# A two-layer decoder trunk on one core: q, k, v, cross-query and memory projections in chunks of 512 columns

## The chip, the core and the metric

The kernel runs on one core of a Trainium2 chip. The core has engines that run side by side, each through its own list of instructions in order: TensorE (matrix products; PE in the profile, with its weight loads as PEld), VectorE (DVE), ScalarE (ACT), GpSimd (POOL) and SyncE (SP), which here only issues DMAs. Data lies in SBUF, results of matrix products in PSUM, which has eight banks of 128 partitions by 512 fp32 numbers. The metric is the device time of one execution in microseconds (us). Lower is better.

## What is computed

Two layers, each on 512 tokens of width 1024, in fp32:

```python
h = rmsnorm(x, g_mix[l])
dq, dk, dv, c_q, c_kv_kr, xq, gate_logits = split(h @ w_in[l])
y_diff = diff_attention(dq, dk, dv, ...) @ w_diff_o[l]        # 8 heads, causal, two softmax maps a head
y_mla  = latent_attention(c_q, c_kv_kr, ...) @ w_mla_o[l]     # 8 heads, causal
mem_n  = rmsnorm(mem, mem_gain[l])                            # 256 memory tokens
y_mem  = memory_cross_attention(xq, mem_n, w_mem_kv[l], ...) @ w_cross_o[l]   # 4 heads
gates  = sigmoid(gate_logits + b_gate[l])                     # three gates
x = x + (gates0*y_diff + gates1*y_mla + gates2*y_mem) @ w_out[l]
u = rmsnorm(x, g_mlp[l]) @ w_mlp1[l]
x = x + square(relu(u)) @ w_mlp2[l]
```

In diff_attention each of q and k is normalized and rotated (rotary) in groups of 64 columns, a head of q or k has two such groups, and a head of v has 128 columns. In the cross-attention q and k are normalized in groups of 128 columns.

## The kernel before

**Precision.** A product of two fp32 matrices is made of three products of a faster type (fp32r). Each operand is split in hi (a rounded copy, ScalarE, line 101 or 105) and lo (the rest, VectorE, line 102 or 106), and `mm3` (lines 108 to 111) issues hi·hi, hi·lo and lo·hi into the same PSUM bank. So almost all of TensorE's work stands on lines 109 to 111, and one product of 128 rows (k) by 128 stationary columns is three matmul instructions, each with a weight load of its own.

**Two forms of projection.** Gates, output projections and the MLP hold 128 columns of the weights stationary and stream all 512 tokens: 512 columns an instruction. The projections of this change (q, k, v, cross-query xq, memory k and v) hold a block of 128 tokens of h stationary and stream weight columns: `chunk256` (lines 259 to 277) does 256 columns of the weights at a time. In it one PSUM bank of the pool `acc` (two banks) takes two token blocks, 256 columns each, so the four token blocks of x need both banks (`tp` 0 and 1) and the two blocks of mem need one. A chunk is two entries, `u` 0 and 1, each with half of the eight k blocks and one weight unit; an entry goes through both banks. At the end of entry 1 `done(tp, bank)` takes the results out: for q and k (`diff_chunk`, lines 552 to 594) a copy on ScalarE (563), squares (565), sums (567), a power on GpSimd (132), rotary on VectorE (582 to 584), the normalization (586), four transposes on TensorE (590) and the split in hi and lo (593); for v a scaled copy (560). There are twelve such chunks a layer for q, k and v (three for each of four pairs of heads), two for xq (`xq_chunk`), and four for the memory (`mem_chunk`).

**Weights.** Each weight unit is at most 128 x 1024 numbers (512 KB). `load_raw` issues its DMA on SyncE into one of RB = 3 raw buffers, `do_split` makes hi and lo in one of NB = 4 pairs of buffers, in the order in which the entries use them. An entry takes its units and gives them back when its matmuls are done (lines 883 to 895). The four lines that fix the order are:

```python
while len(splits) < min(len(units), consumed + NB):
    ...
    do_split()
e.fn(splits[consumed:consumed + n])
```

**Order of the work.** A layer is a list of entries. `merge` mixes attention units (one block of queries of a head or of a pair of heads) with projection entries, phase by phase, as `PLAN` (line 25) says: latent attention with the x gates and the memory projections; then with xq and d0 (q, k and v of head pair 0); cross-attention with d1 and ym; diff attention of pairs 0 to 3 with the rest (gc, d2, d3, gd). A planner then fixes each engine's list: it takes the entries' order as priority and lets a later instruction of an engine go ahead of an earlier one that isn't ready. It also hands out the buffers of each pool: `B` (22 of 128 x 512) for q, k, v and gates, `scr` (5) for the normalization's temporaries, PSUM pools `acc` (2 banks), `s` (3), `tp` (2) and `o` (1).

**Start.** Small inputs come by DMA: `gc` on ScalarE's queue, `posi`, `fr` and `gr` (the q and k gains, which `build_rope` multiplies into the rotary tables), and later `lvt`, on GpSimd's queue (lines 122 to 129 and 185).

Of the kernel before, what the change touches and what calls it, by code (L numbers as in the profile page):

```python
# [15 lines left out]
P = 128  # L16
# [23 lines left out]
class Entry:  # L40
    def __init__(self, fn, units=()):
        self.fn, self.units = fn, list(units)
# [17 lines left out]
def tile_trunk(ctx: ExitStack, tc: tile.TileContext, x_t, mem_t, mem_n, pos, ifr, gcol, grow, w_ck, w_cq, w_kvb, w_qb,  # L60
# [7 lines left out]
    RB, NB = 3, 4  # L68
# [3 lines left out]
    pools = {n: pool(n, b) for n, b in (("H", 16), ("O", 16), ("X", 8), ("G", 1), ("B", 22), ("scr", 5), ("PT", 2))}  # L72
# [52 lines left out]
    G.dma_start(out=posi, in_=pos)  # L125
    fr = ct("fr", [P, 32])
    G.dma_start(out=fr, in_=ifr.partition_broadcast(P))
    gr = ct("gr", [P, L, 128])
    G.dma_start(out=gr, in_=grow[:, 0:128].partition_broadcast(P))
# [8 lines left out]
    dgain = ct("dgain", [P, L])  # L138

    def trig():  # L140
# [44 lines left out]
        G.dma_start(out=lvt.rearrange("p (l d) -> p l d", l=L), in_=grow[:, 128:384].partition_broadcast(P))  # L185
        for l in range(L):
# [8 lines left out]
            V.tensor_scalar(dgain[:, l:l + 1], gc[:, l, C_DO:C_DO + 1], (1.0 - lam_init) * math.sqrt(128.0), None, ALU.mult)  # L195
            V.tensor_scalar(hb[:, l, :], gc[:, l, C_B:C_B + 24], 0.5, None, ALU.mult)
# [3 lines left out]
    def mem_stats():  # L200
# [13 lines left out]
        V.tensor_scalar(mst["eps"], ms, EPS, None, ALU.mult)  # L214
# [44 lines left out]
    def chunk256(units_of, h_of, ntok, done):  # L259
        state = {}  # L260

        def part(u):
            def fn(w):
                hh = h_of()
                if u == 0:
                    state["ps"] = [ps("acc") for _ in range(ntok // 2)]
                for tp in range(ntok // 2):
                    for kk in range(4):
                        k = 4 * u + kk
                        for ti in range(2):  # L270
                            o = state["ps"][tp][:, ti * 256:(ti + 1) * 256]
                            mm3(o, hh(k, 2 * tp + ti), (w[0][0][:, kk, :], w[0][1][:, kk, :]), k == 0 and ti == 0, k == KT - 1 and ti == 1)
                    if u == 1:
                        done(tp, state["ps"][tp])
            return fn

        return [Entry(part(u), [units_of[:, 4 * u:4 * u + 4, :]]) for u in range(2)]

    def layer(l):
# [3 lines left out]
        def build_rope():  # L283
            for qk in range(2):
                a = sm.tile([P, NT, 64], F32, tag=f"ra{qk}", name=nm("ra"), bufs=1)
                b = sm.tile([P, NT, 64], F32, tag=f"rb{qk}", name=nm("rb"), bufs=1)
                for half in range(2):
                    g = gr[:, l, qk * 64 + half * 32:qk * 64 + (half + 1) * 32].unsqueeze(1).broadcast_to([P, NT, 32])
                    G.tensor_tensor(out=a[:, :, half * 32:(half + 1) * 32], in0=cosd, in1=g, op=ALU.mult)
                    G.tensor_tensor(out=b[:, :, (1 - half) * 32:(2 - half) * 32], in0=(sind if half == 0 else nsind), in1=g, op=ALU.mult)  # L290
                s["rope", qk] = (a, b)
# [45 lines left out]

        def mem_chunk(c):
            def done(tp, q):
                if c < 2:  # L340
                    y = tl("scr")
                    A.activation(out=y, in_=q, func=AF.Copy)
                    z = tl("scr")
                    A.activation(out=z, in_=y, func=AF.Square)
                    ss = small("ss", 8, 4)
                    V.tensor_reduce(out=ss[:, :4], in_=z.rearrange("p (g d) -> p g d", d=128), axis=AX.X, op=ALU.add)
                    e = small("e", 8, 4)
                    V.scalar_tensor_tensor(out=e[:, :4].rearrange("p (t h) -> p t h", t=2), in0=ss[:, :4].rearrange("p (t h) -> p t h", t=2), scalar=1.0 / 128,
                                           in1=mst["eps"].unsqueeze(2).broadcast_to([P, 2, 2]), op0=ALU.mult, op1=ALU.add)
                    f = small("f", 8, 4)  # L350
                    rsq(f[:, :4], e[:, :4], 4)
                    yv = y.rearrange("p (g d) -> p g d", d=128)
                    V.tensor_tensor(out=yv, in0=yv, in1=f[:, :4].unsqueeze(2).broadcast_to([P, 4, 128]), op=ALU.mult)
                    tp_ = ps("tp")
                    for h in range(2):
                        for t in range(2):
                            T.transpose(tp_[:, h * 256 + t * P:h * 256 + (t + 1) * P], in_=yv[:, t * 2 + h, :], identity=ident)
                    o = tl("B")
                    scale_to(o, tp_, col(C_CK))
                    s["mk"].append(o)  # L360
                else:
                    o = tl("B")
                    for t in range(2):
                        A.activation(out=o[:, t * 256:(t + 1) * 256], in_=q[:, t * 256:(t + 1) * 256], func=AF.Copy, scale=mst["r"][:, t:t + 1])
                    s["mv"].append(o)
            return chunk256(w_mem[l, c], mem_h, 2, done)
# [610 lines left out]
```

## Time and profile before

| | before |
|---|---|
| time, median of 3 runs | 2054.7 us (2052.78 to 2055.78) |
| span of the profiled execution | 2047.5 us |
| TensorE matmuls (PE) busy | 2025.8 us, 11280 instructions |
| VectorE (DVE) busy | 1125.5 us, 2058 instructions |
| ScalarE (ACT) busy | 870.5 us, 1607 instructions |
| GpSimd (POOL) busy | 152.4 us, 125 instructions |
| HBM read | 175.06 MB, 88 GB/s over the span |

The span is that of one execution, from its first to its last instruction; the time of a run also has what lies around it. A row of matmuls in the views shows the start of one instruction and its own length. Matmuls are pipelined: the next one starts while the one before still runs, so the length of one (0.28 us for 256 columns) is more than it adds to the time. What it adds is read from the distance between two starts.

### The profile page before, as it was taken

What the parts mean: (1) busy time and instruction counts of PE and PEld (TensorE: products, weight loads), DVE (VectorE), ACT (ScalarE), POOL (GpSimd) and SP (SyncE); (2) the same over time, 40 slices, a digit from 0 to 9 for tenths busy, and PEclk for the clock granted to TensorE, in tenths of its full rate; (3) what the DMA queues carried; (4) which work ended last, traced back from release to release, by engine and by line L of the source; (5) the groups of instructions that cost most, each with busy time, mean ns of one, the idle gap of its engine ahead of it and who ended that gap; (6) DMA issues with size and microseconds to landing.
All of it is one profiled execution on the core that took longest, in us unless ns stands there. A gap on an engine that the chain in (4) does not pass through costs nothing.

```text
span 2047.5 us, 28283 instructions
## 1 busy us (share of the span) xinstructions
PE 2025.8 (99%) x11280; PEld 1735.7 (85%) x11280; DVE 1125.5 (55%) x2058; ACT 870.5 (43%) x1607; POOL 152.4 (7%) x125
## 2 busy tenths in 40 slices
PE   8999999999999999999999999999999999999999
PEld 7889997888878888888888999978897788888887
DVE  7754665667656443443457546657685554434442
ACT  6565543444443442322345645444454334323221
POOL 2300110101100000000003001101020000000000
PEclk9999999999999999999999999999999999999999
DMA  5242122222214333333333321212222233333332
GB/s 178 78 140 74 63 65 60 73 73 63 73 48 150 96 97 94 102 93 101 118 95 94 115 72 63 67 58 73 73 63 63 92 124 93 94 102 93 101 94 73
DMA packets 54036, 181.09 MB, mean 88 GB/s; under 512 B 6176, under 2 KB 6704, under 8 KB 53904
## 3 DMA queue, kind: packets, MB, share of 16 engines
q1 hardware_dynamic: 51840, 175.66, 28.0%
q10 hardware_dynamic: 1872, 3.21, 0.5%
q8 instruction: 89, 1.46, 0.3%
q0 software_dynamic: 192, 0.41, 0.1%
q14 instruction: 43, 0.35, 0.1%
HBM read 175.06 MB, written 4.19 MB: 88 GB/s over the span
## 4 chain that ended last, share of the span: by engine, by line
PE 97%; ACT 1%; DMA 1%; DVE 1%; issue 0%; SPq 0%; POOL 0%; POOLq 0%; ACTq 0%
PE psacc L109 21%; PE psacc L110 20%; PE psacc L111 20%; PE pss L109 7%; PE pss L110 7%; PE pss L111 7%; PE pso L642 4%; PE pss L609 3%; PE pss L612 2%; PE pstp L638 2%; PE pstp L649 1%; PE pstp L590 1%; PE pstp L478 1%; DMA X<-in_x_t_dram 0%; DMA B<-in_mem_n_dram 0%; PE pstp L236 0%
## 5 line engine op out<-in xcount | busy, mean ns | idle before, releaser
L101 ACT ACTIVATE whi<-wraw 128x1024 fp32r<-128x1024 f32 (+3 forms) x320 | 334.5, 1047 | 726.8 <-PE psacc L110 354.5
L102 DVE TENSOR_TENSOR wlo<-wraw,whi 128x1024 fp32r<-128x1024 f32 (+3 forms) x320 | 386.0, 1207 | 103.1 <-ACT whi L101 101.8
L109 PE MATMUL psacc<-H,whi 128*128 128x512 f32 x816 | 322.0, 395 | 1.3 <-ACT B L560 1.3
L110 PE MATMUL psacc<-H,whi 128*128 128x512 f32 x816 | 321.1, 393 | 0.0
L111 PE MATMUL psacc<-H,wlo 128*128 128x512 f32 x816 | 319.6, 392 | 0.0
L109 PE MATMUL psacc<-whi,H 128*128 128x256 f32 (+1 forms) x928 | 272.8, 295 | 7.2 <-ACT whi L101 5.8
L110 PE MATMUL psacc<-wlo,H 128*128 128x256 f32 (+1 forms) x928 | 265.9, 287 | 0.5 <-DVE wlo L102 0.5
L111 PE MATMUL psacc<-whi,H 128*128 128x256 f32 (+1 forms) x928 | 265.4, 287 | 0.0
L109 PE MATMUL pss<-O,whi 128*128 128x512 f32 x640 | 249.4, 391 | 1.6 <-ACT O L105 1.6
L110 PE MATMUL pss<-O,whi 128*128 128x512 f32 x640 | 249.7, 390 | 0.0
L111 PE MATMUL pss<-O,wlo 128*128 128x512 f32 x640 | 249.4, 390 | 0.0
L109 PEld LDWEIGHTS psacc<-whi,H 128*128 128x128 f32 x928 | 176.9, 191 | 15.6 <-ACT whi L101 6.0
L109 PEld LDWEIGHTS psacc<-H,whi 128*128 128x128 f32 x816 | 153.3, 188 | 34.7 <-ACT B L560 1.7
L110 PEld LDWEIGHTS psacc<-H,whi 128*128 128x128 f32 x816 | 153.3, 188 | 32.4 <-issue 1.5
L111 PEld LDWEIGHTS psacc<-H,wlo 128*128 128x128 f32 x816 | 153.3, 188 | 32.4 <-issue 1.5
L110 PEld LDWEIGHTS psacc<-wlo,H 128*128 128x128 f32 x928 | 177.6, 191 | 3.2 <-issue 1.4
L111 PEld LDWEIGHTS psacc<-whi,H 128*128 128x128 f32 x928 | 177.0, 191 | 0.0
L808 DVE TENSOR_TENSOR X<-psacc,X 128x512 f32<-128x512 f32 x64 | 44.3, 692 | 207.1 <-PE psacc L111 207.1
L109 PEld LDWEIGHTS pss<-O,whi 128*128 128x128 f32 x640 | 120.0, 188 | 28.3 <-ACT O L105 2.0
L110 PEld LDWEIGHTS pss<-O,whi 128*128 128x128 f32 x640 | 120.2, 188 | 25.2 <-DVE O L106 0.5
L111 PEld LDWEIGHTS pss<-O,wlo 128*128 128x128 f32 x640 | 120.2, 188 | 24.5
L626 ACT ACTIVATE P<-pss,nmx 128x128 f32<-128x128 f32 (+2 forms) x224 | 115.2, 521 | 51.3 <-DVE nmx L623 44.0
(223 smaller groups left out, 3139.6 us busy)
## 6 DMA issues: line engine op xcount, KB each, us to landing
wraw<-in_w_dram SPq DMA_DIRECT2D x128, 512.0 KB, 3.6
wraw<-in_w_g_dram SPq DMA_DIRECT2D x48, 512.0 KB, 3.6
wraw<-in_w_d_dram SPq DMA_DIRECT2D x48, 512.0 KB, 3.8
wraw<-in_w_mem_dram SPq DMA_DIRECT2D x16, 512.0 KB, 3.9
wraw<-in_w_od_dram SPq DMA_DIRECT2D x16, 512.0 KB, 3.5
wraw<-in_w_out_dram SPq DMA_DIRECT2D x16, 512.0 KB, 3.8
X<-in_x_t_dram SPq DMA_DIRECT2D x16, 256.0 KB, 6.3
wraw<-in_w_xq_dram SPq DMA_DIRECT2D x8, 512.0 KB, 3.8
```

The costliest lines, as they stand in the source:

```text
L101: A.activation(out=hi, in_=src, func=AF.Copy)
L102: V.tensor_tensor(out=lo, in0=src, in1=hi, op=ALU.subtract)
L109: T.matmul(o, lhsT=l[0], rhs=r[0], start=first, stop=False)
L110: T.matmul(o, lhsT=l[0], rhs=r[1], start=False, stop=False)
L111: T.matmul(o, lhsT=l[1], rhs=r[0], start=False, stop=last)
L478: T.transpose(tp_[:96, t * P:(t + 1) * P], in_=src[t][:, h * 96:(h + 1) * 96], identity=ident)
L609: T.matmul(sw[m][:, :max(N, 256)], lhsT=qk[m][0][a], rhs=qk[m][1][b], start=i == 0, stop=i == 2)
L612: T.matmul(sv[m], lhsT=qk[m][0], rhs=qk[m][1], start=True, stop=True)
L626: A.activation(out=pt[:, m, :N], in_=sv[m], func=AF.Exp, bias=nmx[:, m:m + 1], accum_out=ssum[m])
L638: T.transpose(tp_[:, n * P:(n + 1) * P], in_=pt[:, m, j * P:(j + 1) * P], identity=ident)
L642: T.matmul(o_out[m], lhsT=w[:, n * P:(n + 1) * P], rhs=vs[m](j), start=j == 0, stop=j == nb - 1)
L808: V.tensor_tensor(out=xt, in0=q, in1=xt, op=ALU.add)
```

## The change

- **Chunks of 512 columns.** `chunk512` takes the place of `chunk256`. A bank of `acc` now holds one token block by 512 columns. For the 512 tokens of x a chunk is four entries: two passes `tp` over pairs of token blocks, each with the two halves `u` of k. A unit is now two k blocks by 512 columns (128 x 1024 numbers as before), so a chunk has four units. They are loaded and split once and kept through both passes: an entry has an offset `off`, a count `need` and a count `take` of units given back, and only the second pass gives back, two units an entry. For the memory (two token blocks) there is one pass.
- **Contents.** A chunk of q and k of a pair of heads (`qk_chunk`, 256 columns of each) and, for every second pair, a chunk of v of two pairs (`v_chunk`): d0 = q, k of pair 0 and v of pairs 0 and 1; d1 = q, k of pair 1; d2 = q, k of pair 2 and v of pairs 2 and 3; d3 = q, k of pair 3. xq is one chunk, the memory two (k, then v).
- **Taking out.** `evict(t, bank)` works on one token block of 512 columns, `done(tp)` does the transposes of a pass. The rotary step multiplies q and k together (two instructions of 512 columns in place of four of 256), and the swap of halves moves from the first product to the sum. The gains of q and k are scaled so that one `tensor_scalar` adds the epsilon for all eight groups (`gr` times 8, `ck11`, and epsilon times 128).
- **Buffers.** NB 4 to 5, `B` 22 to 24, `scr` 5 to 6; the space that GpSimd's DMAs keep is set to 2048.
- **Start.** `posi`, `fr`, `gr` and `lvt` move from GpSimd's queue to ScalarE's; one VectorE instruction scales `gr`.
- The layouts of w_mem, w_xq and w_d are laid for the new units.

```diff
 class Entry:
-    def __init__(self, fn, units=()):
-        self.fn, self.units = fn, list(units)
+    def __init__(self, fn, units=(), off=0, need=None, take=None):
+        self.fn, self.units, self.off = fn, list(units), off
+        self.need = len(self.units) if need is None else need
+        self.take = self.need if take is None else take
...
-    RB, NB = 3, 4
+    RB, NB = 3, 5
...
-    pools = {n: pool(n, b) for n, b in (("H", 16), ("O", 16), ("X", 8), ("G", 1), ("B", 22), ("scr", 5), ("PT", 2))}
+    pools = {n: pool(n, b) for n, b in (("H", 16), ("O", 16), ("X", 8), ("G", 1), ("B", 24), ("scr", 6), ("PT", 2))}
...
-    G.dma_start(out=posi, in_=pos)
+    A.dma_start(out=posi, in_=pos)
...
-    G.dma_start(out=gr, in_=grow[:, 0:128].partition_broadcast(P))
+    A.dma_start(out=gr, in_=grow[:, 0:128].partition_broadcast(P))
+
+    V.tensor_scalar(gr[:, :, 64:128], gr[:, :, 64:128], 8.0, None, ALU.mult)
...
-    def chunk256(units_of, h_of, ntok, done):
+    def chunk512(units_of, h_of, ntok, evict, done):
         state = {}
 
-        def part(u):
+        def part(tp, u):
             def fn(w):
                 hh = h_of()
                 if u == 0:
-                    state["ps"] = [ps("acc") for _ in range(ntok // 2)]
-                for tp in range(ntok // 2):
-                    for kk in range(4):
-                        k = 4 * u + kk
-                        for ti in range(2):
-                            o = state["ps"][tp][:, ti * 256:(ti + 1) * 256]
-                            mm3(o, hh(k, 2 * tp + ti), (w[0][0][:, kk, :], w[0][1][:, kk, :]), k == 0 and ti == 0, k == KT - 1 and ti == 1)
+                    state["ps"] = [ps("acc") for _ in range(2)]
+                for ti in range(2):
+                    q = state["ps"][ti]
+                    for j in range(2):
+                        for kk in range(2):
+                            k = 4 * u + 2 * j + kk
+                            mm3(q, hh(k, 2 * tp + ti), (w[j][0][:, kk, :], w[j][1][:, kk, :]), k == 0, k == KT - 1)
                     if u == 1:
-                        done(tp, state["ps"][tp])
+                        evict(2 * tp + ti, q)
+                if u == 1:
+                    done(tp)
             return fn
 
-        return [Entry(part(u), [units_of[:, 4 * u:4 * u + 4, :]]) for u in range(2)]
+        r, n = [], ntok // 2
+        for tp in range(n):
+            for u in range(2):
+                un = [units_of[:, 4 * u + 2 * j:4 * u + 2 * j + 2, :] for j in range(2)] if tp == 0 else []
+                r.append(Entry(part(tp, u), un, 0 if tp == n - 1 else 2 * u, 2, 2 if tp == n - 1 else 0))
+        return r
...
-        def diff_chunk(p, c):
+        def qk_chunk(p):
+            def evict(t, q):
...
-                for ti in range(2):
-                    yv = y[:, ti * 256:(ti + 1) * 256].rearrange("p (g b d) -> p g b d", g=4, b=2)
...
-                    V.tensor_tensor(out=zv, in0=yv[:, :, ::-1, :], in1=tab(b_), op=ALU.mult)
-                    V.tensor_tensor(out=yv, in0=yv, in1=tab(a_), op=ALU.mult)
-                V.tensor_tensor(out=y, in0=y, in1=z, op=ALU.add)
+                V.tensor_scalar(e, ss, s["ex64"][:, t:t + 1], None, ALU.add)
...
+                V.tensor_tensor(out=v4(z), in0=v4(y), in1=tab(b_), op=ALU.mult)
+                V.tensor_tensor(out=v4(y), in0=v4(y), in1=tab(a_), op=ALU.mult)
+                rv = lambda x: x.rearrange("p (g b d) -> p g b d", g=8, b=2)
+                V.tensor_tensor(out=rv(y), in0=rv(y), in1=rv(z)[:, :, ::-1, :], op=ALU.add)
...
+                s["dy", t] = y
+
+            def done(tp):
...
+                for c in range(2):
+                    tp_ = ps("tp")
...
+                    for h in range(2):
+                        hi, lo = s["d", p, c][h]
+                        split_into(hi[:, sl], lo[:, sl], tp_[:, h * 256:(h + 1) * 256])
+            return chunk512(w_d[l, p + (p > 0) + (p > 2)], x_h, 4, evict, done)
+
+        def v_chunk(vp):
+            def evict(t, q):
+                o = tl("B")
+                A.activation(out=o, in_=q, func=AF.Copy, scale=s["r"][:, t:t + 1])
+                s.setdefault(("dv", vp), []).append(o)
+            return chunk512(w_d[l, (1, 4)[vp]], x_h, 4, evict, lambda tp: None)
...
         def dpair(p):
-            return diff_chunk(p, 0) + diff_chunk(p, 1) + diff_chunk(p, 2)
+            return qk_chunk(p) + (v_chunk(p // 2) if p % 2 == 0 else [])
...
-        mem = sum([mem_chunk(c) for c in range(4)], [])
+        mem = mem_chunk(0) + mem_chunk(1)
...
-        xq = xq_chunk(0) + xq_chunk(1)
+        xq = xq_chunk()
...
-        n = len(e.units)
-        e.fn(splits[consumed:consumed + n])
-        consumed += n
+        assert consumed + e.off + e.need <= len(splits)
+        e.fn(splits[consumed + e.off:consumed + e.off + e.need])
+        consumed += e.take
...
-    nc = _bacc.Bacc("TRN2", target_bir_lowering=False, num_devices=1)
+    nc = _bacc.Bacc("TRN2", target_bir_lowering=False, num_devices=1, dynamic_dma_scratch_size=2048)
```

More of the change, by code (lines that the diff above doesn't have):

```diff
@@ L184, in trig @@
         lvt = tl("B")
-        G.dma_start(out=lvt.rearrange("p (l d) -> p l d", l=L), in_=grow[:, 128:384].partition_broadcast(P))
+        A.dma_start(out=lvt.rearrange("p (l d) -> p l d", l=L), in_=grow[:, 128:384].partition_broadcast(P))
         for l in range(L):
@@ L336, in mem_h, with head_norm @@
             return g
-        def mem_chunk(c):
[L339 to L353, printed above, removed]
+        def head_norm(q, e_of):
+            y = tl("scr")
+            A.activation(out=y, in_=q, func=AF.Copy)
+            z = tl("scr")
+            A.activation(out=z, in_=y, func=AF.Square)
+            ss = small("ss", 8, 4)
+            V.tensor_reduce(out=ss[:, :4], in_=z.rearrange("p (g d) -> p g d", d=128), axis=AX.X, op=ALU.add)
+            e = small("e", 8, 4)
+            V.tensor_scalar(e[:, :4], ss[:, :4], e_of, None, ALU.add)
+            f = small("f", 8, 4)
+            rsq(f[:, :4], e[:, :4], 4)
+            yv = y.rearrange("p (g d) -> p g d", d=128)
+            V.tensor_tensor(out=yv, in0=yv, in1=f[:, :4].unsqueeze(2).broadcast_to([P, 4, 128]), op=ALU.mult)
+            return yv
@@ new lines, in mem_chunk @@
+        def mem_chunk(c):
+            def evict(t, q):
+                if c == 0:
+                    s["my", t] = head_norm(q, mst["eps"][:, t:t + 1])
+                else:
+                    o = tl("B")
+                    A.activation(out=o, in_=q, func=AF.Copy, scale=mst["r"][:, t:t + 1])
+                    s["mv"].append(o)
+            def done(tp):
+                if c == 0:
+                    for hp in range(2):
+                        tp_ = ps("tp")
+                        for h in range(2):
+                            for t in range(2):
+                                T.transpose(tp_[:, h * 256 + t * P:h * 256 + (t + 1) * P], in_=s["my", t][:, 2 * hp + h, :], identity=ident)
+                        o = tl("B")
+                        A.activation(out=o, in_=tp_, func=AF.Copy, scale=ck11[:, l:l + 1])
+                        s["mk"].append(o)
+            return chunk512(w_mem[l, c], mem_h, 2, evict, done)
@@ L354, in done, with x_h, xq_chunk @@
+        def x_h():
+            return lambda k, t: tok(s["h"], k, t)
+        def xq_chunk():
+            def evict(t, q):
+                s["xy", t] = head_norm(q, s["ex128"][:, t:t + 1])
+            def done(tp):
+                if tp == 0:
+                    s["xq"] = [tl("B") for _ in range(4)]
+                for hp in range(2):
                     tp_ = ps("tp")
@@ L356, in done @@
                         for t in range(2):
[L357 to L365, printed above, removed]
@@ L396, in ck_item @@
+                            T.transpose(tp_[:, h * 256 + t * P:h * 256 + (t + 1) * P], in_=s["xy", 2 * tp + t][:, 2 * hp + h, :], identity=ident)
+                    for h in range(2):
+                        scale_to(s["xq"][2 * hp + h][:, tp * 256:(tp + 1) * 256], tp_[:, h * 256:(h + 1) * 256], col(C_CQ))
+            return chunk512(w_xq[l], x_h, 4, evict, done)
         def ck_item(w):
@@ L568, in done @@
                 e = small("e", 8, 4)
-                sv, ev = (a.rearrange("p (t g) -> p t g", t=2) for a in (ss, e))
-                bc = lambda a: a[:, 2 * tp:2 * tp + 2].unsqueeze(2).broadcast_to([P, 2, 4])
-                if c == 0:
-                    V.tensor_tensor(out=ev, in0=sv, in1=bc(s["ex64"]), op=ALU.add)
-                else:
-                    V.scalar_tensor_tensor(out=ev, in0=sv, scalar=1.0 / 64, in1=bc(s["epsx"]), op0=ALU.mult, op1=ALU.add)
+                V.tensor_scalar(e, ss, s["ex64"][:, t:t + 1], None, ALU.add)
```

98 lines of the change are left out of this document (38 added, 60 removed).

## The prediction

> **What bounds the kernel now.** I read the page first: its engines and the chain that ended last.
>
> ```profile
> span 2047.5 us, 28283 instructions
> PE 2025.8 (99%) x11280; PEld 1735.7 (85%) x11280; DVE 1125.5 (55%) x2058; ACT 870.5 (43%) x1607; POOL 152.4 (7%) x125
> ...
> PE 97%; ACT 1%; DMA 1%; DVE 1%; issue 0%; SPq 0%; POOL 0%; POOLq 0%; ACTq 0%
> ```
>
> TensorE is busy for 99% of the span and makes 97% of the chain, so the time is the sum of what its matmuls add, and other engines count only where they make it wait. But a busy time made of pipelined rows doesn't say what one matmul adds. So next came the groups by form, for the number of instructions that the change touches:
>
> ```profile
> L109 PE MATMUL psacc<-whi,H 128*128 128x256 f32 x896 | 263.2, 294 | 1.4 <-ACT scr L563 1.4
> L111 PE MATMUL psacc<-whi,H 128*128 128x256 f32 x896 | 256.6, 287 | 0.0
> L110 PE MATMUL psacc<-wlo,H 128*128 128x256 f32 x896 | 255.8, 286 | 0.0
> ...
> L109 PE MATMUL psacc<-whi,O 128*128 128x256 f32 x128 | 38.2, 299 | 0.5 <-ACT O L105 0.5
> ```
>
> The chunks are 3 x 896 matmuls with h (H) and 3 x 128 with mem (O), 3072 of 256 columns. Then the timeline of TensorE, for the distance between starts: a run of 384 columns (14 rows from the first to the last shown), one in the xq stage (31 rows), one in the MLP (25 rows). The first and the last matmul of the kernel stand around them.
>
> ```profile
> 5.61 0.85 PE L109 MATMUL psacc<-whi,H 128*128 128x288 f32 x2 [5.61 <-ACT whi L101]
> ...
> 61.06 0.33 PE L110 MATMUL psacc<-wlo,B 128*128 128x384 f32 x1
> ...
> 63.32 0.33 PE L111 MATMUL psacc<-whi,B 128*128 128x384 f32 x1
> ...
> 200.07 0.28 PE L111 MATMUL psacc<-whi,H 128*128 128x256 f32 x1
> ...
> 203.67 0.28 PE L111 MATMUL psacc<-whi,H 128*128 128x256 f32 x1
> ...
> 700.64 0.39 PE L110 MATMUL pss<-O,whi 128*128 128x512 f32 x1
> ...
> 706.08 0.39 PE L110 MATMUL pss<-O,whi 128*128 128x512 f32 x1
> ...
> 2043.28 0.39 PE L111 MATMUL psacc<-B,wlo 128*128 128x512 f32 x1
> ```
>
> Steps: 3.60 / 30 = 0.1200 us for 256 columns, 2.26 / 13 = 0.1738 for 384, 5.44 / 24 = 0.2267 for 512. 256 more columns cost 0.1067, and 0.1067 + 0.0133 is the 256 step: each matmul carries about 13.3 ns that don't depend on its columns. The 384 columns lie on the same line (0.160 + 0.0133 = 0.1733 against 0.1738).
>
> **The change part by part.**
>
> *Matmuls.* 3072 of 256 columns become 1536 of 512. Before they add 3072 x 0.1200 = 368.6 us; after, 1536 x 0.2267 = 348.2. **-20.5 us**, all on TensorE's path. The weight loads halve with them (11280 to 9744), beside the matmuls. Transposes and attention stay in number.
>
> Here a rule speaks against the change. The Trainium skill's TensorE: Matmul & The Clock Gate, section Back-to-back issue gap, gives a warm matmul N/2.4 + 2.5 ns. By it a pair would save only 2.5 ns, 3.8 us over 1536 pairs. The trace's two steps give 13.3 in place of 2.5, so the sum goes by the trace.
>
> *Taking out.* The widths change and the count doesn't: four evictions for 512 columns of weights and all tokens as before.
>
> ```profile
> L582 DVE TENSOR_TENSOR scr<-scr,rb 128x256 f32<-128x256 f32 x64 | 24.2, 420 | 0.0
> L583 DVE TENSOR_TENSOR scr<-scr,ra 128x256 f32<-128x256 f32 x64 | 24.1, 414 | 0.0
> ...
> L586 DVE TENSOR_TENSOR scr<-scr,f 128x512 f32<-128x512 f32 x32 | 22.0, 692 | 6.1 <-POOL f L132 6.1
> ```
>
> Rotary: 128 instructions (48.3 us) become 64 of 512 columns at 692 ns (44.3): -4.0 us of VectorE. The swapped read moves from a row of 420 ns to the sum; beside the unswapped 414 it costs nothing to speak of. None of this is on TensorE's path: worth 0 as long as matmuls cover it.
>
> *PSUM.* Bank 0 of a pass is complete 12 matmuls (2.72 us) before the pass ends, before it was 24 x 0.120 = 2.88 us. The copy that frees a bank:
>
> ```profile
> L563 ACT ACTIVATE scr<-psacc 128x512 f32<-128x512 f32 x32 | 18.9, 592 | 20.3 <-PE psacc L111 17.1 <-DVE scr L582 3.2
> ```
>
> 0.59 us, and ScalarE waited for TensorE there (17.1), seldom for a free `scr` (3.2), which gets a sixth buffer. Cost 0; cover left 2.1 us.
>
> *Weights.* Units keep their size and number. What is new is that four of five pairs of buffers are held through 72 of a chunk's 96 matmuls. When the first half of pass 2 gives back two, 24 matmuls (5.44 us) are left. In that time two units must be made:
>
> ```profile
> L102 DVE TENSOR_TENSOR wlo<-wraw,whi 128x1024 fp32r<-128x1024 f32 x306 | 374.0, 1223 | 100.1 <-ACT whi L101 99.1 <-PE pstp L420 0.7
> ...
> L101 ACT ACTIVATE whi<-wraw 128x1024 fp32r<-128x1024 f32 x306 | 324.0, 1060 | 707.0 <-PE psacc L110 344.5 <-PE pss L110 213.5 <-issue 72.2
> ```
>
> The next chunk begins with the fifth pair, ready long before, and the first of these two: 1.06 + 1.22 = 2.28 us after release, inside 5.44. The fourth is released at the chunk's end and needed 5.44 us later. ScalarE sat 344.5 + 213.5 us before this line because it waited for TensorE to free buffers: splitting is ahead of need. Behind a waiting split ScalarE's later copies queue, as they do today. I take 0. The bounds: -2 us (the fifth buffer ends small waits for splits elsewhere) and 2.28 a boundary if nothing covers it; 7 chunks of four entries a layer, 14 boundaries, +31.9.
>
> *VectorE in the stage of d3.* Head pair 3's chunks run beside diff attention of pair 2. d3 loses its v chunk (11.5 us of TensorE with next to no VectorE work), which moves to the stage before. The windows of that stage in both layers, and of the d1 stage:
>
> ```profile
> 480.00:530.00 50.00, 48.66 (x347) 43.63 (x347) 39.24 (x96) 25.80 (x60) 16.13 (x13) 1.00 0.22 64
> 1496.00:1546.00 50.00, 48.66 (x347) 43.63 (x347) 38.59 (x96) 25.75 (x60) 11.79 (x5) 1.00 0.20 64
> ...
> 250.00:300.00 50.00, 49.51 (x389) 48.10 (x389) 30.85 (x60) 24.50 (x55) 9.89 (x4) 1.00 0.21 64
> ```
>
> TensorE (second number) idles 1.34 us in 50; VectorE (fourth) has 39.24. Of the 50 us, 288 matmuls of d3 are 34.6 and 1.3 idle, so 14.1 are attention and transposes. After: 96 x 0.2267 + 14.1 = 35.9 us of TensorE against 39.24 - 2 units of v (2.45) - rotary (0.5) = 36.3 of VectorE. The margin is gone. Below, nothing is lost if gate matmuls of the next stage step in, and the stage of d2, which gained 21.8 - 11.5 us of light work, gives slack; a gain isn't excluded, and -1 a layer stands as that end. Above, count the demand with nothing moved out of the stage, by the rows of its parts (of the four widths of 623 and 632 the widest and the narrowest):
>
> ```profile
> L621 DVE TENSOR_TENSOR pss<-pss,mask 128x128 f32<-128x128 f32 x160 | 45.8, 295 | 71.0 <-PE pss L609 55.3 <-PE pss L612 13.6 <-PE pstp L638 1.6
> ...
> L623 DVE TENSOR_REDUCE nmx<-pss 128x1 f32<-128x512 f32 x48 | 32.6, 685 | 0.4
> ...
> L102 DVE TENSOR_TENSOR B<-pstp,B 128x256 fp32r<-128x256 f32 x64 | 26.4, 420 | 15.1 <-ACT B L101 14.7
> ...
> L567 DVE TENSOR_REDUCE ss<-scr 128x8 f32<-128x512 f32 x32 | 21.6, 676 | 2.3 <-ACT scr L565 2.3
> ...
> L632 DVE SCALAR_TENSOR_TENSOR P<-P,c 128x512 f32<-128x512 f32 x16 | 12.0, 748 | 0.4
> ...
> L623 DVE TENSOR_REDUCE nmx<-pss 128x1 f32<-128x128 f32 x32 | 8.6, 283 | 0.2
> ...
> L632 DVE SCALAR_TENSOR_TENSOR P<-P,c 128x128 f32<-128x128 f32 x16 | 5.6, 349 | 0.4
> ...
> L535 DVE TENSOR_SCALAR e<-ss,eq 128x4 f32<-128x4 f32 x16 | 3.6, 222 | 0.0
> ```
>
> For a head: 8 masks (2.4), two reductions at each width (4 x 2 x 0.48 = 3.9), the combination of both maps (632, 2.2), its scalars and the closing steps (630, 631, 646, 720 to 723 and 106, some 3.9): 12.4, so 24.7 for two. For the chunk: four evictions of 0.68 + 0.22 + 4 x 0.69, eight splits of 0.42 and four units of 1.22, 23.0. That is 47.7 against 35.9, 11.8 us a layer. The nearest row is the stage's own idle, 1.34; I take that it doubles: **+2.7 us** for both layers. The d1 stage has 30.85 of 50 and stays below 80% by the same count.
>
> *Start.*
>
> ```profile
> 0.74 0.41 ACTq L123 DMA_DIRECT2D gc<-in_gcol_dram  x1
> ...
> 3.74 0.63 ACT L223 ACTIVATE scr<-X 128x512 f32<-128x512 f32 x1 [1.28 <-DMA X<-in_x_t_dram]
> ...
> gr<-in_grow_dram POOLq DMA_DIRECT2D x1, 128.0 KB, 8.2
> gc<-in_gcol_dram ACTq DMA_DIRECT2D x1, 58.0 KB, 3.2
> ```
>
> Three more issues of 0.41 on ScalarE ahead of its first work fit the 1.28 us it waits for x. What queues behind them is the split of the first weights. The new VectorE instruction on `gr` waits for that DMA; if it stands ahead of the first h split and `gr` lands as now (issued at 3.00, 8.2 later: 11.2 us), about 6 us are lost; landing like `gc` (3.2), nothing. I take 0, the nearer row. `lvt` is one more issue on ScalarE, 0.41, under matmuls.
>
> **Sum.** -20.5 + 2.7 = -17.8. The profiled span goes from 2047.5 to 2029.7. The median of the runs lies 7.2 above the span; taken as unchanged, 2054.7 - 17.8 = **2036.9 us**.
>
> **The rivals.**
>
> *VectorE rules the d3 stage (0.17).* Full price 2 x 11.8 = 23.6: 2054.7 - 20.5 + 23.6 = 2057.8; half, 2046. For it: the stage's 78% of VectorE today beside idle of TensorE. Against: five gates can fill, and the planner lets them.
>
> *Weights late at chunk boundaries (0.06), the slower side.* The first matmul of each chunk waits for its second unit because one spare pair is too few when the evictions of the last pass stand ahead of the splits on both engines. Price 2.28 at 14 places: 2054.7 - 20.5 + 31.9 = 2066.1. It loses from 1.46 us a boundary on. Against it:
>
> ```profile
> PE psacc L109 <- ACT whi L101: 5.8, 2, 5.6
> ...
> PE psacc L110 <- DVE wlo L102: 0.5, 2, 0.3
> ```
>
> In the waits of TensorE, splits made it wait 5.8 us, of which 5.6 is the start, and 0.5.
>
> *The change doesn't do what it says: the step isn't paid per matmul (0.03).* If the 13.3 ns went with the operands' 256 columns and not with the instruction, the new step would be twice the old one, 0.240, and nothing would be saved: 2054.7. Against: three widths and three sets of operands lie on one line. The Trainium skill's formula above would take this side with 3.8 us saved, 2050.9.
>
> *Idle goes too (0.07).* Of 21.7 us of TensorE's idle (2047.5 - 2025.8), 5.6 are before the first matmul and about 4 after the last; half of the rest gone with the new buffers, and no loss at d3: 2054.7 - 20.5 - 6 = 2028.
>
> **How the numbers follow.** The forecast, 2030 to 2043, has 0.66; the last 0.01 is a start that loses 6 us with another loss. 2028 to 2050 holds 0.66, half of the idle case and most of the VectorE case, about 0.8. This kernel's measurement tells 0.2% (4.1 us) from no change: faster means below 2050.6, same up to 2058.8. Faster: 0.66 + 0.07 + 0.11 of the VectorE case = 0.84; same: its other 0.06, 0.03 and 0.01 = 0.10; slower 0.06.
>
> **What would show it.** Steps of 0.2267 us in the chunks and 9744 matmuls: the main term. A wait of TensorE for `whi` or `wlo` that repeats with each chunk: the weights rival. In the window of d3, VectorE above 90% with TensorE idle growing by more than 1.4 us a layer: the second rival. First matmul later than 5.6 us: the start. The forecast is wrong if 512-column matmuls in the chunks step at more than 0.232, or if TensorE's idle grows by more than 10 us.

## The result and the profile after

The change made the kernel slower by 0.9%. The forecast was 2036.9 us, with a range of 2028 to 2050.

| | before | after |
|---|---|---|
| time, median of 4 runs each | 2054.36 us (2052.78 to 2055.78) | 2069.55 us (2068.01 to 2075.41) |
| ratio | | 1.0091, 95% interval 1.0074 to 1.0107 |
| span of the profiled execution | 2047.5 us | 2066.2 us |
| TensorE idle (span less busy) | 21.7 us | 47.4 us |
| mean granted clock of TensorE | 1.000 | 0.993 |

The head of the page of the kernel after, its engines and its chain that ended last:

```profile
span 2066.2 us, 25130 instructions
PE 2018.8 (98%) x9744; PEld 1656.8 (80%) x9744; DVE 1126.1 (54%) x1997; ACT 870.8 (42%) x1587; POOL 163.0 (8%) x121
...
PE 94%; ACT 2%; DVE 2%; DMA 1%; issue 1%; POOL 0%; ACTq 0%; DVEq 0%; POOLq 0%
```

The number of matmuls is what the change says, 9744. But TensorE's idle time has grown by 25.7 us, and its share of the chain has fallen from 97% to 94%. Two rows of its timeline, the first and the last of 17 matmuls that follow each other in the xq stage:

```profile
200.19 0.40 PE L113 MATMUL psacc<-whi,H 128*128 128x512 f32 x1
...
203.84 0.39 PE L112 MATMUL psacc<-wlo,H 128*128 128x512 f32 x1
```

3.65 / 16 = 0.228 us a step: a chunk's matmuls cost what was forecast. So the loss is in waits. The waits of TensorE after, in us in total, times and longest:

```profile
PE pstp L662 <- DVE scr L659: 12.5, 6, 4.9
PE pstp L651 <- DVE B L104: 8.0, 5, 3.4
PE psacc L111 <- ACT whi L103: 6.9, 1, 6.9
PE pso L655 <- ACT PT L97: 5.8, 8, 0.8
PE psacc L111 <- ACT scr L566: 5.6, 10, 0.9
```

The same view of before has

```profile
PE pstp L649 <- DVE scr L646: 2.8, 4, 0.8
PE psacc L109 <- ACT B L560: 2.3, 4, 0.6
...
PE pso L642 <- ACT PT L95: 1.5, 4, 0.5
PE psacc L109 <- ACT scr L563: 1.4, 2, 0.7
```

The longest wait before, the start apart, was 0.8 us (line 649, which is 662 now; 642 is 655 now). Now there are two kinds of stop, 3.4 and 4.9 us long, and each comes in both layers.

**The first stop** lies behind the second qk chunk (d1). The timeline after, in order of time (start, length, engine, what, and in brackets the idle time before it):

```profile
292.74 0.82 PE L596 MATMUL pstp<-ident,scr 128*128 128x128 f32 x6
293.29 1.06 ACT L103 ACTIVATE whi<-wraw 128x1024 fp32r<-128x1024 f32 x1 [0.90 <-PE pstp L596]
...
294.25 0.37 ACT L103 ACTIVATE B<-pstp 128x256 fp32r<-128x256 f32 x1
294.38 1.22 DVE L104 TENSOR_TENSOR wlo<-wraw,whi 128x1024 fp32r<-128x1024 f32 x1 [0.73 <-ACT whi L103]
295.52 0.42 DVE L104 TENSOR_TENSOR B<-pstp,B 128x256 fp32r<-128x256 f32 x1
...
296.96 0.63 PE L651 MATMUL pstp<-ident,P 128*128 128x128 f32 x4 [3.40 <-DVE B L104]
```

The eight transposes of the last pass (line 596) fill both `tp` banks. The splits that empty these (`B<-pstp`) stand behind splits of weights on ScalarE (1.06 us) and on VectorE (1.22 us). Attention's next transposes need a `tp` bank. They stand first in TensorE's list, so it stops for 3.40 us.

**The second stop** lies at the tail of diff attention:

```profile
581.11 0.69 DVE L749 TENSOR_TENSOR B<-psacc,R 128x512 f32<-128x512 f32 x1 [0.20 <-PE psacc L113]
...
582.81 0.97 PE L622 MATMUL pss<-B,B 64*128 64x384 f32 x6
583.14 0.59 ACT L672 ACTIVATE scr<-pso 128x512 f32<-128x512 f32 x1
...
586.83 1.01 POOL L136 TENSOR_TENSOR of<-e,mhalf 128x4 f32<-128x4 f32 x1 [27.15 <-DVE e L736]
587.88 0.69 DVE L659 TENSOR_TENSOR scr<-scr,of 128x512 f32<-128x512 f32 x1 [1.19 <-POOL of L136]
...
588.72 1.09 PE L662 MATMUL pstp<-ident,scr 128*128 128x128 f32 x4 [4.93 <-DVE scr L659]
```

The first row takes out the last of the eight gates that the plan keeps for the end of attention. With it TensorE's other work is used up. The chain that closes head 6 (copy, squares, sum, power, normalization) begins at 583.14, and its transposes wait 4.93 us for it. The timeline of before has the same rows as

```profile
575.96 0.69 DVE L646 TENSOR_TENSOR scr<-scr,of 128x512 f32<-128x512 f32 x1 [0.52 <-POOL of L132]
...
582.85 0.69 DVE L736 TENSOR_TENSOR B<-psacc,R 128x512 f32<-128x512 f32 x1 [3.92 <-PE psacc L111]
```

There the head closed 6.9 us ahead of the last gate; now it closes 6.8 us behind it.

**The clock.** Windows of after (TensorE, weight loads, VectorE, ScalarE, GpSimd, then the granted clock). The first lies behind the first stop, the second has the tail's stop in it, the third is a stretch without a stop, the fourth lies behind the tail's stop of layer 1:

```profile
300.00:302.00 2.00, 2.00 (x7) 1.64 (x7) 0.18 (x1) 0.53 (x3) 0.00 (x0) 0.50 0.00 0
586.00:595.00 9.00, 5.55 (x16) 3.81 (x17) 4.26 (x10) 3.39 (x10) 1.01 (x1) 0.50 0.07 28
570.00:580.00 10.00, 10.00 (x59) 7.76 (x58) 5.92 (x17) 5.09 (x13) 0.00 (x0) 1.00 0.16 54
1613.00:1623.00 10.00, 9.13 (x24) 6.62 (x25) 4.04 (x10) 3.81 (x11) 0.00 (x0) 0.50 0.00 0
```

Behind each stop the granted clock is halved. In the timeline the steps show it:

```profile
594.49 0.63 PE L113 MATMUL pss<-O,wlo 128*128 128x512 f32 x1
594.92 0.63 PE L111 MATMUL pss<-O,whi 128*128 128x512 f32 x1
...
596.46 0.39 PE L113 MATMUL pss<-O,wlo 128*128 128x512 f32 x1
596.69 0.39 PE L111 MATMUL pss<-O,whi 128*128 128x512 f32 x1
```

0.43 us from the first to the second, 0.23 from the third to the fourth. The trace has the clock halved for 3.4 us (from 298.8 us on), 10.2 (585.5), 6.8 (1319.4) and 10.2 (1612.9), 30.7 us together. TensorE was idle in 6.7 of them, where a halved clock costs nothing. In the other 24.0 us half was lost: an estimate of 12.0 us of matmul time. So a stop is paid twice: by itself and by the slow matmuls behind it.

**The ledger.** The span is 36.5 us above the forecast's 2029.7. The named waits grew by 9.7 (line 662), 8.0 (651), 4.3 (655), 1.9 (copies of `acc`, 5.6 against 2.3 + 1.4) and 1.5 (start), 25.4 together, of which 2.7 were granted in the forecast. With the 12.0 of the clock this makes 34.7; the other 1.8 us are not assigned to a wait.

### The profile page after: what moved, and what is told of

Read it like the earlier page. It is cut to its first block, busy times and chain, and to the rows that moved or that the text cites. A ratio compares the mean times of both kernels' runs of the same rounds, so it can differ in the third digit from the quotient of the medians.

```text
span 2066.2 us, 25130 instructions
## 1 busy us (share of the span) xinstructions
PE 2018.8 (98%) x9744; PEld 1656.8 (80%) x9744; DVE 1126.1 (54%) x1997; ACT 870.8 (42%) x1587; POOL 163.0 (8%) x121
## 4 chain that ended last, share of the span: by engine, by line
PE 94%; ACT 2%; DVE 2%; DMA 1%; issue 1%; POOL 0%; ACTq 0%; DVEq 0%; POOLq 0%
PE psacc L111 20%; PE psacc L113 19%; PE psacc L112 19%; PE pss L111 7%; PE pss L112 7%; PE pss L113 7%; PE pso L655 4%; PE pss L622 3%; PE pstp L651 2%; PE pss L625 2%; PE pstp L662 1%; PE pstp L489 1%; PE pstp L596 1%; DVE wlo L104 1%; ACT whi L103 0%
## 5 line engine op out<-in xcount | busy, mean ns | idle before, releaser
L104 DVE TENSOR_TENSOR wlo<-wraw,whi 128x1024 fp32r<-128x1024 f32 (+3 forms) x320 | 386.2, 1208 | 115.1 <-ACT whi L103 114.5
L111 PE MATMUL psacc<-whi,H 128*128 128x512 f32 (+1 forms) x480 | 190.3, 400 | 9.6 <-ACT whi L103 6.9
L112 PE MATMUL psacc<-wlo,H 128*128 128x512 f32 (+1 forms) x480 | 186.7, 390 | 0.9 <-DVE wlo L104 0.9
L113 PE MATMUL psacc<-whi,H 128*128 128x512 f32 (+1 forms) x480 | 185.7, 391 | 0.0
L136 POOL TENSOR_TENSOR f<-e,mhalf 128x8 f32<-128x8 f32 (+1 forms) x60 | 113.0, 1887 | 393.8 <-DVE e L572 210.6
L807 DVE SCALAR_TENSOR_TENSOR scr<-pss,R 128x512 f32<-128x512 f32 x64 | 43.9, 691 | 160.5 <-PE pss L113 154.1
L655 PEld LDWEIGHTS pso<-B,PT 128*128 128x128 f32 x768 | 102.9, 194 | 19.1 <-ACT PT L97 9.2
```

What stands on the lines that cost most here:

```text
L104: V.tensor_tensor(out=lo, in0=src, in1=hi, op=ALU.subtract)
L111: T.matmul(o, lhsT=l[0], rhs=r[0], start=first, stop=False)
L112: T.matmul(o, lhsT=l[0], rhs=r[1], start=False, stop=False)
L113: T.matmul(o, lhsT=l[1], rhs=r[0], start=False, stop=last)
L136: G.tensor_tensor(out=o, in0=e, in1=mhalf[:, :n], op=ALU.pow)
L655: T.matmul(o_out[m], lhsT=w[:, n * P:(n + 1) * P], rhs=vs[m](j), start=j == 0, stop=j == nb - 1)
```

## The experiments

Theory A: the 512-column matmuls save what was forecast, but the change leaves the plan's entries as they were while their sizes change (d0 and d2 now carry a whole v chunk, d1 and d3 none), so that some stages run out of matmuls and TensorE stops; each stop halves the clock. Theory B: the buffers that the passes need (`scr`, PSUM) are what runs short. Theory C: the softmax chains are too long for what is left to cover them. In some of the expectations theory A is called F; theory V there says that VectorE has too much to do in these stages, wherever the matmuls stand.

**Gates beside d3.** The plan alone:

```diff
-"d2 gc", "d3", "gd:5", "gd"
+"d2 gc:3", "d3 gc", "gd:5", "gd"
```

> Only the plan is changed: three entries of the cross gates go from the stage of d2 to that of d3, so that gate matmuls stand behind the chunk of q and k there. After the change TensorE stops for 4.9 us, waiting for the scaled head output in line 659, near 584 and 1608 us, and the granted clock is halved for 10.2 us each time. Theory F (no matmuls are left that wait for nothing): this stop goes or falls below 2 us, the clock isn't halved there, the span falls by 10 to 18 us from 2066.2; the other stop, 3.4 us near 293 and 1317, stays. Theory V (VectorE's work in these stages is too much, wherever the matmuls stand): the stop moves but the span stays within 4 us.

2066.09 us (span 2064.3, clock 0.994). Its waits of TensorE, and the timeline and a window further on in layer 1:

```profile
PE pstp L651 <- DVE B L104: 9.6, 5, 3.6
...
PE pstp L662 <- DVE scr L659: 2.6, 4, 0.8
```

```profile
1373.19 0.66 PE L662 MATMUL pstp<-ident,scr 128*128 128x128 f32 x4 [0.80 <-DVE scr L659]
1374.53 0.55 PE L111 MATMUL psacc<-O,whi 128*128 128x512 f32 x1 [0.58 <-ACT O L103]
```

```profile
1372.00:1386.00 14.00, 12.63 (x43) 8.85 (x40) 8.72 (x24) 5.64 (x18) 0.00 (x0) 0.63 0.00 1
```

The stop at the tail is gone, as theory A has it: three gate items more beside d3 leave gates of the last kind for the tail (their matmuls run up to 590 us). But the span fell by 1.9 us only, as theory V had it. TensorE's idle time fell from 47.4 to 39.7 us, and its busy time grew from 2018.8 to 2024.6. The clock was halved in other places, the longest time (10.2 us) behind two waits of 0.80 and 0.58 us.

**v0 behind q1.** The qk and v chunks as groups of their own, and the plan:

```diff
-"xq d0", "d1 ym", "gc:6", "d2 gc", "d3", ...
+"xq q0", "q1 v0 ym", "gc:6", "q2 v1 gc", "q3", ...
```

> Only the order is changed: the chunk of v for pairs 0 and 1 goes from behind q, k of pair 0 to behind q, k of pair 1, where the kernel before had a v chunk too. Theory F: the stop of 3.4 us near 293 and 1317 us, where the transposes of line 651 wait for the split in line 104, goes, the clock isn't halved there, and the span falls by 8 to 14 us; the stop near 584 stays. Theory B (the buffers scr and the PSUM pool tp are what holds up the evictions): the stop stays, at 2 us or more.

2058.05 us (span 2056.3, clock 0.995). The waits of TensorE:

```profile
PE pstp L662 <- DVE scr L659: 10.9, 4, 4.9
...
PE pstp L651 <- DVE B L104: 1.8, 4, 0.6
```

The first stop is gone, and the clock stays whole there; the tail's stop stays, with its halved clock. That is 9.9 us of span for one of the two stops.

**More scr.** Eight buffers for six, with one raw weight buffer less:

```diff
-    RB, NB = 3, 5
+    RB, NB = 2, 5
-... ("scr", 6) ...
+... ("scr", 8) ...
```

> scr has 8 buffers in place of 6; the room comes from the raw weight buffers, 2 in place of 3. Theory B: the copies of line 566 out of the PSUM pool acc no longer come 11 us late in the stage of d1, the stop near 293 falls below 1.5 us, the span falls by 6 to 14 us. Theory F: the stop near 584 stays at 4 us or more and the span stays within 6 us of 2066.2; a loss of a few us by the missing raw buffer is possible under both.

2071.94 us (span 2070.2, clock 0.992). Both stops are there, the first one 5.2 us long now. The missing raw buffer may have added to it, and this run doesn't tell the two apart. But two more buffers of `scr` ended neither stop, and the run before this one ended the first with the six as they were. For `scr`, theory B isn't borne out.

**Both orders together**, with the scaling of `gr` moved behind the rotary angles:

```diff
+"xq q0", "q1 v0 ym", "gc:6", "q2 v1 gc:3", "q3 gc", "gd:5", "gd"
...
             if l == 0:
                 trig()
+                V.tensor_scalar(gr[:, :, 64:128], gr[:, :, 64:128], 8.0, None, ALU.mult)
```

> Both changes of order together, and the scaling of gr moved from the start of VectorE's list to the place where the rotary tables are made, since it held up the first split of weights by 1.4 us. Theory F: both stops go, the clock stays at 1.000, the first 20 us lose 1 to 1.5 us less, and the span is 2030 to 2040, below that of the kernel before. Theory V or B: 2050 or more.

2048.47 us, median of 10 (2045.62 to 2055.58), against 2049.86 of the kernel before, median of 13; ratio 0.9996, interval 0.9985 to 1.0008. The profiled execution has a clock of 1.000 and a span of 2044.3 us: without the stops 21.9 us come back. That is the larger part of what was lost, and the expectation (2030 to 2040) was still missed. VectorE's work is the same as in the changed kernel, so theory V falls with the stops. Its waits of TensorE:

```profile
PE pso L654 <- ACT PT L97: 8.2, 12, 1.1
PE psacc L111 <- ACT whi L103: 7.0, 1, 7.0
PE psacc L111 <- ACT scr L565: 4.6, 8, 1.0
PE pstp L650 <- DVE B L104: 4.2, 4, 1.4
```

No stop is left, but many waits around 1 us. The start is as late as after the change, because the planner put the scaling first again.

**No gates kept back, in the kernel before.**

```diff
-"gd:5", "gd"
+"gd", ""
```

> The kernel before the change with only its plan altered: all eight gates of the last kind beside the last two attention heads, none kept for behind them, so nothing covers the chain that closes the last head. Theory (a stop of TensorE comes from missing cover, and the stop halves the granted clock): a wait of 4 to 5.5 us for the closing chain in each layer, the clock halved for about 10 us each time, span 2064 to 2072 where it was about 2048. Rival (the stops belong to the 512-column passes): no wait over 1.5 us, clock 1.000, span within 3 us of 2048.

2053.02 us (span 2051.2, clock 0.999); its longest wait for a closing chain is 0.8 us. A miss for theory A as I had put it: where the plan names the gates doesn't decide, since the planner still finds some for the tail. What decides is whether head 6 closes ahead of the last gate. That can be read in every kernel here, the rows being those of 575.96 and 582.85 us above, and both layers agree. Where the head closes first (the kernel before, this run, and seven of the others), no wait for a closing chain is over 1.1 us. Where the last gate comes first (the changed kernel and v0 behind q1 above; more scr, the first run with v1 beside heads 0 and 1, three accumulator banks, and half of the transposes later alone), the longest is 2.9 to 4.9 us.

**Shorter chains.** The two instructions that add the mask are left out, in the kernel with both orders and in the one before:

```diff
-                    V.tensor_tensor(out=dg, in0=dg, in1=mask, op=ALU.add)
```

> The changed kernel in both new orders, with the causal mask left out of the MLA and the differential scores (each wide unit has two VectorE instructions of 0.3 us less between scores and exponentials; rows above the diagonal count). Theory (what is left over of the loss is the attention chains, which fewer projection matmuls cover): TensorE's waits fall by 8 us or more, span 2033 to 2037. Rival (waits come from the in-order queues of ScalarE and from the banks, not from the chains' length): span falls by less than 4 us, 2040 or more.

> The kernel before the change with the causal mask left out in the same places. Theory of the chains: its larger number of projection matmuls already covers them, so the span falls by 1 to 4 us, clearly less than in the changed kernel. Rival: both kernels fall by the same.

Spans 2044.4 (2044.3 with the mask) and 2045.3 us, one run each. The changed kernel gains nothing from shorter chains: TensorE waits 7.8 us for `PT` and 5.5 for `B L104`, against 8.2 and 4.2 with the mask. Theory C isn't borne out. Beside it the kernel before ran with a span of 2049.8 us, so it gained 4.5; but its spans lie between 2046.2 and 2056.3 us in the other runs, and a single run doesn't show that gain.

**Small loads on GpSimd.** `posi`, `fr`, `gr` and `lvt` as before the change, `gr` scaled by GpSimd, otherwise both orders:

```diff
-    A.dma_start(out=gr, in_=grow[:, 0:128].partition_broadcast(P))
+    G.dma_start(out=gr, in_=grow[:, 0:128].partition_broadcast(P))
```

> The changed kernel in both new orders, with the four small loads issued by GpSimd as before the change and the scaling of the gain rows done by GpSimd. Theory (the start lost 1.3 us to ScalarE's four issues ahead of its table load and 1 to 1.6 us to VectorE's wait for the gain rows): first matmul back at 5.6 us, no early wait for wlo, span 2041 to 2043 against 2044.3. Rival (the second loss is taken up by later waits): first matmul at 5.6, span 2043 to 2045.

2046.78 us (span 2045.0, clock 0.997). The wait of the first matmul is 5.6 us again, the one for `wlo` is gone, and everything up to 480 us lies 3.7 us earlier. The clock took it back: it was halved for 3.4 and 6.8 us, with TensorE idle in 0.7 of them, which is worth some 4.8 us. Both stretches begin behind a wait of 1.4 us for `B L104`; behind the same waits in the run with both orders the clock stayed whole.

**Stages filled evenly.** On top of that, v1 beside heads 0 and 1:

```diff
-"gc:6", "q2 v1 gc:3", "q3 gc"
+"v1 gc:3", "q2 gc:4", "q3 gc"
```

> The version with the small loads on GpSimd, and the stages filled more evenly: the second v chunk and three gate items beside heads 0 and 1, the third qk chunk and four items beside heads 2 and 3, the fourth and five items beside heads 4 and 5 (7, 8 and 9 entries in place of 6, 11 and 7). Theory (what is left of the loss is uneven filling: attention falls behind in the full stage and TensorE waits in the thin one): the waits for PT, B and scr fall by 4 us or more together, no halved clock, span 2037 to 2041. Rival (the rest is the planner's order inside the stages and doesn't hang on how many entries a stage has): span 2043 to 2047.

> The same with 6, 7 and 11 entries: two more gate items kept for the stage of heads 4 and 5, where VectorE has most to do for the time TensorE is given. By the theory of uneven filling it lies between the last one and the version before it, 2039 to 2044; if the fourth qk chunk's own demand on VectorE is what counts, it is the best, 2036 to 2040. By the rival again 2043 to 2047.

The second has `"v1 gc:2", "q2 gc:3", "q3 gc"`. 2068.66 us, ratio 1.0093 (1.0076 to 1.011), and 2057.42, ratio 1.0041 (1.0026 to 1.0056). Both are worse than both cases I had put: the spans are 2065.7 and 2056.0 us, where the rival had up to 2047. The first has waits of 3.9 us at a new place (`pss L621 <- ACT P L638`, in both layers), 2.9 us for the closing chain of head 6 again, and a clock of 0.991. That the number of entries in a stage can be balanced on paper falls.

**Three accumulator banks**, two for scores, on the kernel with both orders:

```diff
-("acc", 2), ("s", 3)
+("acc", 3), ("s", 2)
```

> The changed kernel in both new orders with three accumulator banks and two score banks in place of two and three. If the turn of the two accumulator banks is a cost (a pass of two token blocks holds both, and the next pass begins as the first is copied out), the waits of psacc for the copy fall from 4.6 us to under 1 and the span by 3 to 5 us, to about 2040. Rival: the banks are free in time and the wait comes from what stands ahead of the copy on ScalarE; the span stays or grows by up to 10 us, since attention has a bank less.

2080.22 us (span 2078.4, clock 0.985). The wait for copies of `acc` is 5.2 us, not under 1: the third bank doesn't help it. The stops are back (17.5 us for the closing chains) in a run in which attention has a score bank less. For the accumulator banks theory B falls too.

**Half of the transposes later.** With both orders and the small loads on GpSimd; of the eight transposes behind a pass of a qk chunk the second four are issued one entry later:

```diff
-                for c in range(2):
-                    tp_ = ps("tp")
+                def half(c):
+                    tp_ = ps("tp")
...
+                half(0)
+                pend.append(lambda: half(1))
...
         e.fn(splits[consumed + e.off:consumed + e.off + e.need])
+        if held and pend == held and e.units:
+            for f in pend:
+                f()
+            pend.clear()
```

> The version with both new orders and the small loads on GpSimd; in the qk chunks the second four of the eight transposes that follow each pass are issued one entry (5.44 us) later, so that the chunk holds one tp bank at a time and not both. Theory (the waits left over, and the halved clock they bring, come from both tp banks held while their splits stand behind weight splits on VectorE): the waits of the P transposes for that split fall from 4.2 us to under 1.5, no halved clock, span 2037 to 2041. Rival (another wait takes its place, since scr tiles are held longer or the chains are late anyway): span 2043 or more.

**2041.33 us**, median of 7 (2040.92 to 2043.01), against 2050.52 of before, median of 9; ratio **0.9954**, interval 0.994 to 0.9968. It is the one version that is faster than both kernels by more than the noise, and its expectation held (span 2039.1 us). Its waits of TensorE:

```profile
PE pso L662 <- ACT PT L97: 6.0, 8, 1.1
PE psacc L111 <- ACT whi L103: 5.6, 1, 5.6
PE psacc L111 <- ACT scr L569: 5.0, 8, 1.0
```

The wait for `B L104` has gone from the list, and the clock is 1.000. The span is 5.9 us below that of the run with the small loads on GpSimd, of which some 4.8 are the halved clock of that one run. The two groups of transposes of one pass stand 4.3 us apart in its timeline:

```profile
485.99 0.49 PE L601 MATMUL pstp<-ident,scr 128*128 128x128 f32 x3
...
490.34 0.60 PE L601 MATMUL pstp<-ident,scr 128*128 128x128 f32 x4
```

**The same alone**, on the changed kernel with its own plan and start:

> The changed kernel with its plan and start as they are; only the second four transposes after each pass of a qk chunk are issued one entry later. Theory (the stop at the second qk chunk is both tp banks held until splits that stand behind weight splits): the stop of 3.4 us near 297 and 1320 us goes (under 1.5) and with it the halved clock behind it; the stop of 4.9 us at the tail of attention stays, with about 10 us of halved clock each; span 2053 to 2059 where the changed kernel had 2066.2. Rival (the stop is due to what the plan puts beside that chunk, and the banks only show it): it stays at 3 us or more, or another wait of that size takes its place, span 2063 or more.

2069.75 us, ratio 1.0088 (1.0059 to 1.0117), span 2069.9. Neither case came in full. The wait for the splits fell from 3.4 to 2.0 us in both layers. In layer 0 the clock behind it was halved all the same, for 6.8 us; in layer 1, behind the same wait of 2.01 us at 1326.08, it stayed whole. Most of the halved time lies at the tail now, 13.7 us in layer 0 and 17.1 in layer 1, where TensorE waits up to 4.2 us for the chain of head 6. In this plan TensorE has nothing else there: both groups of transposes end up beside each other (the last four rows of line 602 start at 295.43, 1.4 us behind the three at 294.05). So the held banks are one part of the first stop. That no matmul is ready beside them is the other: with v0 behind q1 there was one, and the longest wait was 0.6 us.

## Why the prediction was wrong, step by step

The step that failed is the count of TensorE's waits. The sum allowed 2.7 us for them, and TensorE's idle time grew by 25.7; and an idle stretch was priced at its own length, while the clock behind it cost some 12 us more.

**Matmuls, -20.5: right.** Number and step are as forecast, 9744 and 0.228 us. The step stands against the 0.216 us that the formula of the Trainium skill's page TensorE: Matmul & The Clock Gate (Back-to-back issue gap) gives for 512 columns, there as the gap of an isolated matmul; the measurement decides here.

**Weights, 0: the rival was wrong, and so was the step.** TensorE never waited for `whi` or `wlo` behind the start, so weights aren't late. What failed is the sentence "Behind a waiting split ScalarE's later copies queue, as they do today. I take 0." The price of two units given back at once wasn't that the units come late, but that the splits of q and k, and with them both `tp` banks, queue behind them: 3.4 us in each layer, in a stage (d1) that I had dismissed by its VectorE share. Without the plan's part in it (v0 behind q1) the longest of these waits is 0.6.

**VectorE in the stage of d3, +2.7: the demand was right, the place and the price were wrong.** The windows after, in layer 0:

```profile
480.00:530.00 50.00, 47.94 (x245) 37.32 (x244) 41.40 (x96) 24.83 (x54) 11.07 (x7) 1.00 0.19 62
...
500.00:530.00 30.00, 27.94 (x148) 22.04 (x147) 27.40 (x62) 17.22 (x37) 8.16 (x6) 1.00 0.22 71
```

VectorE is at 91% for 30 us, as the sign demanded, but TensorE's idle there is only 2.06 us against 1.34. "Five gates can fill, and the planner lets them" was true, and it was counted as an argument against the rival. It was the mechanism: by the close of head 5 five of the eight gates were out (at 559.71 us), before the change three (at 546.16). The two were missing from 584 us on, where the closing chain of head 6 had nothing beside it. The price is the tail's 4.9 us a layer. With three more gate items beside d3 that stop is gone.

**The clock: not in the sum at all.** Every row of before that I read had a granted clock of 1.00, and none shows what a stop of TensorE does to it. I priced idle time at its own length. By the estimate above some 12 us of the gap are this.

**Start, 0: mis-sized.** The timeline after:

```profile
2.13 0.46 ACTq L131 DMA_DIRECT2D gr<-in_grow_dram  x1
3.72 1.28 ACT L107 ACT_TABLE_LOAD   x1 [3.72 <-DMA X<-in_x_t_dram]
...
8.15 0.23 DVE L133 TENSOR_SCALAR gr<-gr 128x128 f32<-128x128 f32 x1 [1.62 <-DMA gr<-in_grow_dram]
...
9.10 0.61 PE L112 MATMUL psacc<-wlo,H 128*128 128x288 f32 x1 [0.88 <-DVE wlo L104]
```

The issues did fit in the wait for x, as I wrote. But the load of ScalarE's function table, which had stood in that wait (at 1.18 us), moved behind it: the first matmul came at 6.88 us in place of 5.61. And `gr` held up the first split of weights for 0.88. Together 2.1 us, and 1.5 more than the waits of before (6.9 + 0.9 against 5.8 + 0.5), within my bounds of 0 and 6; the small loads back on GpSimd gave back both.

**PSUM, 0: mis-sized.** The copies of `acc` cost 1.9 us more; the banks are not the reason, as the third one didn't shorten the wait.

**The base, 2054.7 us: a wrong reading.** I took the 7.2 us between the median and the span of the profiled run as what lies around a span. In every later run a time lies 1.7 to 1.8 us above its own span. The profiled run had a clock of 1.000; later runs of the kernel before at 2053 to 2058 us had 0.995 to 0.997. So some halved clock was probably in the 2054.7 already, though the clocks of those first runs aren't on record.

**What is still open.** The best version's span is 9.4 us above the forecast's 2029.7, and this isn't in its named waits (20.8 us against 18.0 before, about the 2.7 that were granted). By its page TensorE is busy for 2013.6 us, 12.2 less than before and not 20.5. The rows of both traces say where the rest is, each counted from its start to the next start, but not beyond its own end. The chunks' matmuls take 391.0 us before and 366.4 in the best version: 24.6 less, so the main term came in full. The other matmuls of `mm3` take 1349.5 and 1351.2. The small matmuls of attention and the transposes take 284.9 and 295.6: 10.7 more (303.0 in the changed kernel, a part of it by the clock), though their number and sizes are the same. Why they follow each other more slowly isn't shown; a wait shorter than the row before it would count as busy time here.

## What to carry to other kernels

When a change makes the work of the bounding engine shorter, it also takes away what covers the chains of the other engines: count for each stage what is left to cover them, and look for the price at the end of the pool from which a short stage is filled, not in that stage. When chunks change in size, their order has to be made anew, and tried: here moves of a few entries in the plan alone shifted the time between 2046.8 and 2068.7 us, and filling the stages evenly on paper gave the upper end. Idle time of TensorE isn't worth its own length: read the granted clock behind each stop.

## What the runs showed of the hardware

Behind stops of 3.4 to 4.9 us the granted clock of the changed kernel fell to 0.50, for up to 10 us, and steps of 512 columns went from 0.23 to 0.43 us. The Trainium skill's page TensorE: Matmul & The Clock Gate, section HAM oscillation, has the rule that no gap of TensorE should be over some 3.4 us. The stops agree with it. But in the run with gates beside d3 the clock fell behind two waits of 0.80 and 0.58 us (0.63 over 14 us), so staying under that gap was not enough here. Nor does the same wait always do it: behind 2.01 us the clock was halved in one layer and whole in the other (half of the transposes later, alone), and behind 1.4 us it was halved with the small loads on GpSimd and whole with both orders. The kernel before is near this edge too: beside the runs with the new orders it took from 2048.24 to 2057.31 us, the latter at a mean clock of 0.995.
